# Ten pairs of projection blocks by Strassen's seven products, in a fused mLSTM, attention and feed-forward step

## The chip, the cores and the metric

The kernel runs on one core of one Trainium2 chip. TensorE (PE) multiplies, VectorE (DVE), ScalarE (ACT) and GpSimd (POOL) do the element-wise work, and SyncE (SP) issues most DMAs. Products are accumulated in PSUM; ACT and DVE read them from there. The metric is the device time of one launch, in microseconds (us), as the median of several runs. Times inside a launch come from one execution recorded by the hardware profiler.

## What is computed

One step of a hybrid decoder layer, for a prompt of 1024 tokens and a sample group of 8 x 4 tokens (1056 columns in all), with a model width of 1024. Cut to what matters:

```python
h = _ln(x) * (1.0 + sc1) + sh1
z = h @ w_in + b_in                       # one projection of all kinds
qm, km, vm, ig, fg, og, qa, ka, va, gm, ga = _split(z, IN_SPLITS)
hm, C, n, m = _mlstm(qm, km, vm, ig, log_sigmoid(fg), C0, n0, m0)   # 4 heads, chunks of 128 tokens
hm = _ln(hm) * mlstm_norm_w * sigmoid(og)
ha, k_new, v_new = _swa(qa, ka, va, kbuf, vbuf, pos0, sinks)        # 16 heads, window 128
merged = sigmoid(gm) * (hm @ w_branch_m) + sigmoid(ga) * (ha @ w_branch_a)
x = _ln(ALPHA * x + g1 * (merged @ w_out), ln1_g, ln1_b)
h2 = _ln(x) * (1.0 + sc2) + sh2
f, cbuf_new = _conv_ffn(h2, cbuf, w_up, b_up, conv_w, conv_b, w_down, b_down)
x = _ln(ALPHA * x + g2 * f, ln2_g, ln2_b)
# in _mlstm, per chunk: smat = (q k^T) * exp(dmat - mt); num = smat v + a_in * (C q); C = decay * C + k^T (ws v)
```

All data are float32.

## The kernel before

**Products.** Features stand on the partitions and tokens along the free axis. A block is 128 output features over all 1056 tokens. `group` (L442) makes the products of a block for one token tile of `TT` (384, 384 and 288 columns). Weights and activations are each split into two fp32r parts, hi and lo, and of the four partial products three are made (hi hi, hi lo, lo hi): for eight slices of the contraction 24 matmuls for a tile, 72 for a block. `Stream` (`win`) loads the weights of coming blocks on SP (`wraw`, L403), and ACT (L424) and DVE (L428) split them.

**Phases.** Phase A: the projection, 52 blocks of the kinds k, q, v, og (mLSTM), qa, ka, va (attention), gm, ga (branch gates) and the narrow gate rows. Phase B: two branch products and the output product. Phase C: feed-forward, `up` blocks and `down` blocks, where DVE adds each down group to a sum in SBUF (L1680). Some later stages follow.

**Side work.** mLSTM (a generator `mlstm(h)` for each head), attention (`swa_pair`, `swa`) and gate arithmetic are steps in the queue `sides`. `group` calls `pulse` after each slice; `pulse` advances a clock of products' time and takes a step from the queue whenever clock times rate (`RATES`) says so. A step issues all its instructions on every engine at once, so its PE instructions stand in one piece between two slices of a block. `finish_sides` takes all that are left, with nothing between them, before the last block of phase A. `later` puts off a DMA by some of that clock.

**PSUM.** It has eight tiles of 512 columns: `L[0..2]` for the direct groups, handed out in turn by `lbank`; `PD[0..1]`, `PE_`, `PF` and `PG` for side work. In an mLSTM step, chunk s is prepared in `PE_` (scores `k q`, L799, and three transposes), read by DVE and ACT (L804 to L810); `hn` (L751) of chunk s-2 is read by ACT out of `PD[(s-2) % 2]`; `hn` of s-3 is transposed into `PG` and multiplied by DVE (L824); the products of s-1 (L789) go to `PD[(s-1) % 2]` and `PF`. In an attention step the scores of two heads go to `PD[0]`, of two to `PD[1]` (L1137), each copied by ACT (L1142) and DVE (L1143); exponentials on ACT (L1122) of the step before stand ahead of these copies. An instruction that writes a tile waits, by semaphores that the framework puts in, for those that still read it.

**Slots.** SBUF has 43 slots of 128 x 1056 floats, handed out in the order in which they came back; an instruction that takes a slot waits for its last user.

Of the kernel before, what the change touches and what calls it, by code (L numbers as in the profile page):

```python
# [11 lines left out]
F32 = mybir.dt.float32  # L12
# [38 lines left out]
# columns of the table of constants  # L51
# [52 lines left out]
def hybrid_step(ctx: ExitStack, tc: tile.TileContext, I, O):  # L104
# [25 lines left out]
    def drop(*ts):  # L130
        for t in ts:
            free_slots.append(tag_of.pop(id(t))[0])
# [57 lines left out]
    # the rows of c in pieces of 128  # L190
# [7 lines left out]
    # vectors along the features, transposed: 0.. b_in (16 + 36 blocks), 52.. b_ada, 100.. norm_w,  # L198
    # 108.. b_down, 116.. b_up, 160.. conv_b, 204.. conv_w (3 x 44)
# [22 lines left out]
    def ada_load(ca, cb, f0, n=256):  # L222
        """Features f0 .. f0 + n of the factors ca and cb: their weights."""
        out = []
        for c in (ca, cb):
            for hf in range(2):
                if n > 128 or not hf:
                    t = slot(name="wada")
                w = t[:, hf * 512:hf * 512 + 512] if n == 128 else t[:, :1024]
                S.dma_start(w.rearrange("p (k c) -> p k c", k=4),  # L230
                            dap(W_ADA, hf * 4 * 128 * 6 * D + c * D + f0,
                                [[6 * D, 128], [128 * 6 * D, 4], [1, n]]))
                out.append((t, w))
        return out
# [32 lines left out]
    # silu(c), transposed  # L267
# [109 lines left out]
    def h_lo(k, ti, eng):  # L377
        t0, nt = TT[ti]
        hi, lo = acts[k]
        c = slice(t0, t0 + nt)  # L380
        eng.tensor_tensor(lo[:, c], h_f[k][0][:, c], hi[:, c].bitcast(F32), op=OP.subtract)
        h_f[k][1] += 1
        if h_f[k][1] == 3:
            drop(h_f.pop(k)[0])

# [1 line left out]
    class Stream:  # L387
        def __init__(self, specs):
            self.specs = specs
            self.raws, self.parts, self.loaded = {}, {}, 0  # L390

        def load(self, upto):
            while self.loaded <= min(upto, len(self.specs) - 1):
# [12 lines left out]
                self.loaded += 1  # L406

        def prep(self, i, later_lo=False):
            if i >= len(self.specs) or i in self.parts:
                return  # L410
# [43 lines left out]
    # ================= phase A: the combined projection, mLSTM, window attention =================  # L454
# [11 lines left out]
    for h in range(4):  # L466
        blk("k", h, 512 + 128 * h)
        blk("q", h, 128 * h)
        if h == 0:
            order.append(("gate", 0))  # L470
            specs.append(("gate",))
        blk("v", 2 * h, 1024 + 256 * h)
        blk("v", 2 * h + 1, 1024 + 256 * h + 128)
        blk("og", 2 * h, 2056 + 256 * h)
        blk("og", 2 * h + 1, 2056 + 256 * h + 128)
    gates = [("gm", j, 4616 + 128 * j) for j in range(8)] + [("ga", j, 5640 + 128 * j) for j in range(8)]
    gates = deque(gates)

    def add_gates(n):
        for _ in range(n):  # L480
            blk(*gates.popleft())
# [5 lines left out]
    blk("ka", 0, 4104)  # L487
    blk("va", 0, 4360)
    add_qa(0)
    add_gates(3)  # L490
    add_qa(1)
    add_gates(2)
    blk("ka", 1, 4104 + 128)
    blk("va", 1, 4360 + 128)
    add_qa(2)
    add_gates(4)
    add_qa(3)
    add_gates(7)

    # the order of all later products: branches, output product, feed-forward  # L500
# [25 lines left out]
    win = Stream(specs)  # L526

    # the first products take the chunks of h as they come
# [64 lines left out]
    # later constants  # L593
    v2, v3, v4 = slot(name="v2"), slot(name="v3"), slot(name="v4")
    rows(v2, 0, I["b_up"], 0, 44)
    rows(v2, 44, I["conv_b"], 0, 44)
    rows(v3, 0, I["conv_w"], 0, 88)
    rows(v4, 0, I["conv_w"], 88 * 128, 44)
# [7 lines left out]
    def late_consts():  # L606
        transpose(PF[:, 0:88], v2[:88, :128], 88)
# [105 lines left out]
    def cache_load(p):  # L713
        """The cached keys and values of a pair of groups."""
# [21 lines left out]
    def norm_tail(num, den, ecol, n):  # L736
        """The layer norm of num / max(|den|, e): its factor is (var(num) + eps max(|den|, e)^2)^-0.5."""
# [37 lines left out]
        # operands in two parts: q, v with a column of ones, the scores and the weighted keys  # L775
# [68 lines left out]
        # the state after the prompt  # L844
# [6 lines left out]
        # the sample group: all its tokens as one block  # L851
# [145 lines left out]
    def swa(g):  # L997
# [37 lines left out]
        def sample():  # L1035
            """The sample group: its rows are (sequence, head, token)."""
# [158 lines left out]
    def gate_rows_in(i):  # L1195
        """The gates' rows: products with both parts of the weights side by side, then their sum."""
# [47 lines left out]
    for h in range(4):  # L1244
        after["og", 2 * h + 1] = [lambda h=h: mlstm(h)]
    after["og", 7].append(state_n_out)
# [5 lines left out]
    def raw_pieces(src, ti):  # L1252
        """Loads a token tile of eight blocks that wait in DRAM."""
# [10 lines left out]
    def refill(raws, ti):  # L1264
        """Puts a token tile into the operand tiles, whose old contents its products have used."""
# [9 lines left out]
    rate[0] = RATES[0]  # L1275
    for i, (kind, idx) in enumerate(order):
        last = i == len(order) - 1
        if (kind, idx) == ("k", 1):
            rate[0] = RATES[1]
        if (kind, idx) == ("ka", 0):  # L1280
            rate[0] = RATES[2]
# [25 lines left out]
    # ================= phase B: branches and output product =================  # L1307
# [192 lines left out]
    # ================= phase C: the convolutional feed-forward =================  # L1500
# [14 lines left out]
    def conv_piece(c, y, a, b, w0):  # L1515
        """The prompt's columns a..b of the convolution of block c."""
# [20 lines left out]
    def post(c):  # L1537
        """Convolution, then gelu or the product, of a block that is complete."""
# [22 lines left out]
    def post_now(c, ti):  # L1561
        """The same for the last block, a token tile at a time."""
# [16 lines left out]
    def history():  # L1579
        """What the convolution reads of earlier steps, by feature; space for what it keeps."""  # L1580
# [24 lines left out]
    def pre():  # L1605
        """ALPHA x and the gated sums of all groups but the last, by tokens, into DRAM."""
# [26 lines left out]
        # the last gate along the features, on every token's partition: the prompt's, the samples'  # L1633
# [18 lines left out]
    def spread(gen, us):  # L1652
        """The steps of gen, one every us of the products' time."""
# [31 lines left out]
    # the first blocks take the token tiles in the order in which their norms end  # L1685
# [201 lines left out]
```

## Time and profile before

| | us |
|---|---|
| median of 3 runs | 1983.2 |
| the runs | 1982.83 to 1986.43 |
| span of the profiled execution | 1981.8 |
| PE busy in it | 1942.6 (98%) |
| DVE busy | 997.7 (50%) |
| ACT busy | 723.3 (36%) |
| POOL busy | 308.9 (16%) |

The profiled execution's span lies 1.4 us under the median. Names such as `L450` are lines of the kernel before; `L` among the tiles, as in `L<-hhi,whi`, is any of the three direct banks. The ends of matmuls are modelled, so spacings are read from start to start. [...]

### The profile page before, as it was taken

What the parts mean: (1) busy time and instruction counts of PE and PEld (TensorE: products, weight loads), DVE (VectorE), ACT (ScalarE), POOL (GpSimd) and SP (SyncE); (2) the same over time, 40 slices, a digit from 0 to 9 for tenths busy, and PEclk for the clock granted to TensorE, in tenths of its full rate; (3) what the DMA queues carried; (4) which work ended last, traced back from release to release, by engine and by line L of the source; (5) the groups of instructions that cost most, each with busy time, mean ns of one, the idle gap of its engine ahead of it and who ended that gap; (6) DMA issues with size and microseconds to landing.
All of it is one profiled execution on the core that took longest, in us unless ns stands there. A gap on an engine that the chain in (4) does not pass through costs nothing. (4 is left out here: it accounts for less than half of the span.)

```text
span 1981.8 us, 31279 instructions
## 1 busy us (share of the span) xinstructions
PE 1942.6 (98%) x12597; PEld 1858.1 (94%) x12597; DVE 997.7 (50%) x2166; ACT 723.3 (36%) x1522; POOL 308.9 (16%) x592
## 2 busy tenths in 40 slices
PE   6999999999999999999999999999999999999996
PEld 4899999999998989999999999999999999999995
DVE  4454444444544535241454455564554554645579
ACT  4534334343546445331312454353131312222331
POOL 2013223231123131200000333100000000000007
PEclk9999999999999999999999999999999999999998
DMA  9151424324220322497524142111212020211533
GB/s 289 47 140 25 140 35 119 84 70 100 69 76 23 112 72 60 136 345 244 159 65 128 54 129 67 36 38 48 60 35 62 28 69 27 63 34 49 194 130 130
DMA packets 214362, 187.86 MB, mean 95 GB/s; under 512 B 8849, under 2 KB 197953, under 8 KB 214185
## 3 DMA queue, kind: packets, MB, share of 16 engines
q1 hardware_dynamic: 213437, 185.26, 31.1%
q8 instruction: 98, 1.61, 0.3%
q10 hardware_dynamic: 780, 0.61, 0.1%
q14 instruction: 47, 0.39, 0.1%
HBM read 150.06 MB, written 37.81 MB: 95 GB/s over the span
## 5 line engine op out<-in xcount | busy, mean ns | idle before, releaser
L450 PE MATMUL L<-hhi,whi 128*128 128x384 f32 (+1 forms) x1600 | 526.4, 329 | 0.1
L450 PE MATMUL L<-hlo,whi 128*128 128x384 f32 (+1 forms) x1600 | 517.0, 323 | 0.0
L450 PE MATMUL L<-hhi,wlo 128*128 128x384 f32 (+1 forms) x1600 | 516.5, 323 | 0.0
L450 PE MATMUL L<-mhi,whi 128*128 128x384 f32 (+1 forms) x1248 | 407.4, 326 | 4.9 <-DVE r L1466 3.0
L450 PE MATMUL L<-mhi,wlo 128*128 128x384 f32 (+1 forms) x1248 | 404.1, 324 | 0.4 <-DVE wlo L428 0.4
L450 PE MATMUL L<-mlo,whi 128*128 128x384 f32 (+1 forms) x1248 | 403.3, 323 | 0.0
L428 DVE TENSOR_TENSOR wlo<-wraw,whi 128x1024 fp32r<-128x1024 f32 (+1 forms) x148 | 174.5, 1180 | 331.3 <-ACT whi L424 330.8
L450 PEld LDWEIGHTS L<-hhi,whi 128*128 128x128 f32 x1600 | 301.5, 188 | 6.6 <-issue 4.8
L450 PEld LDWEIGHTS L<-hlo,whi 128*128 128x128 f32 x1600 | 301.9, 189 | 0.3
L450 PEld LDWEIGHTS L<-hhi,wlo 128*128 128x128 f32 x1600 | 301.4, 188 | 0.0
L450 PEld LDWEIGHTS L<-mhi,whi 128*128 128x128 f32 x1248 | 235.4, 189 | 6.7 <-DVE r L1466 3.3
L450 PEld LDWEIGHTS L<-mhi,wlo 128*128 128x128 f32 x1248 | 234.9, 188 | 1.0 <-DVE wlo L428 1.0
L450 PEld LDWEIGHTS L<-mlo,whi 128*128 128x128 f32 x1248 | 235.3, 189 | 0.1
L1511 ACT ACTIVATE u<-L,vT 128x384 f32<-128x384 f32 (+1 forms) x132 | 71.8, 545 | 378.6 <-PE L L450 378.6
L424 ACT CAST whi<-wraw 128x1024 fp32r<-128x1024 f32 (+1 forms) x148 | 149.2, 1009 | 28.3 <-DMA wraw<-in_w_up 25.3
L450 PE MATMUL L<-ahi,whi 128*128 128x384 f32 (+1 forms) x432 | 139.9, 324 | 0.0
L450 PE MATMUL L<-ahi,wlo 128*128 128x384 f32 (+1 forms) x432 | 139.4, 323 | 0.0
L450 PE MATMUL L<-alo,whi 128*128 128x384 f32 (+1 forms) x432 | 139.3, 323 | 0.0
L1524 DVE SCALAR_TENSOR_TENSOR y<-u,vT,y 128x1023 f32<-128x1023 f32 (+3 forms) x92 | 113.7, 1235 | 2.5
L1534 POOL COPY ucol<-u 128x2 f32<-128x2 f32 x44 | 10.3, 234 | 631.7 <-ACT u L1511 631.7
L1680 DVE TENSOR_TENSOR facc<-L,facc 128x384 f32<-128x384 f32 (+1 forms) x120 | 62.7, 522 | 58.6 <-PE L L450 58.4
L298 POOL TENSOR_SCALAR rstd<-mv 128x1 f32<-128x1 f32 (+1 forms) x36 | 22.0, 611 | 400.6 <-DVE mv L307 377.2
(422 smaller groups left out, 2652.4 us busy)
## 6 DMA issues: line engine op xcount, KB each, us to landing
wraw<-in_w_in SPq DMA_DIRECT2D x52, 512.0 KB
wada<-in_w_ada SPq DMA_DIRECT2D x44, 512.0 KB
wraw<-in_w_up SPq DMA_DIRECT2D x44, 512.0 KB
wraw<-in_w_down SPq DMA_DIRECT2D x24, 384.0 KB
hD<-og SPq DMA_DIRECT2D x8, 528.0 KB
gmD<-gm SPq DMA_DIRECT2D x8, 528.0 KB
haD<-ha SPq DMA_DIRECT2D x8, 528.0 KB
gaD<-ga SPq DMA_DIRECT2D x8, 528.0 KB
```

The source lines that it names most:

```text
L298: G.tensor_scalar(r[:n], var, eps, None, op0=OP.add)
L424: A.copy(hi[:, :n], t[:, :n])
L428: V.tensor_tensor(lo[:, :n], t[:, :n], hi[:, :n].bitcast(F32), op=OP.subtract)
L450: T.matmul(ps[:, :nt], x[:, c], y[:, t0:t0 + nt], start=i == 0, stop=i == last)
L1511: A.activation(u[:, t0:t0 + n], ps[:, :n], AF.Identity, bias=b)
L1524: V.scalar_tensor_tensor(y[:, f:b], u[:, f - d:b - d], w[i], y[:, f:b], op0=OP.mult, op1=OP.add)
L1534: G.tensor_copy(aux["ucol"][:, c, 0:2], u[:, SEQ - 2:SEQ])
L1680: V.tensor_tensor(fx, ps[:, :nt], fx, op=OP.add)
```

## The change

Twenty blocks (four of gm, eight v, eight og) are no longer made directly. They are taken in ten pairs of two neighbouring blocks, and a pair is one 2 x 2 block product (two output blocks, even and odd slices of the contraction, two halves of the tokens) by Strassen's scheme in Winograd's form: seven products of half size instead of eight, over sums of weights (`Pair.step`, DVE) and of activations (`tprep`). Each product is 24 matmuls of 264 columns into each half of one PSUM tile; DVE and ACT add the products up out of PSUM (U1 to U5, `put`). To that end PSUM is now four tiles of 1024 columns, and the old banks are their halves.

The order is new: four gm blocks directly, the ten pairs (`fast`), the gate rows, then 28 direct blocks (k and q of the heads with ga blocks between, ka, va, qa), beside which all of mLSTM and attention runs at one rate. v and og are stored to DRAM after their pair (`pD`) and loaded again by `mlstm(h)`.

```diff
-    L = [psum.tile([128, 512], F32, name=f"L{i}") for i in range(3)]
-    PD = [psum.tile([128, 512], F32, name=f"PD{i}") for i in range(2)]
-    PE_, PF, PG = (psum.tile([128, 512], F32, name=f"P{i}") for i in "EFG")
+    BK = [psum.tile([128, 1024], F32, name=f"B{i}") for i in range(4)]
+    L = [BK[0][:, :512], BK[0][:, 512:], BK[1][:, :512]]
+    PD = [BK[2][:, :512], BK[2][:, 512:]]
+    PE_, PF, PG = BK[1][:, 512:], BK[3][:, :512], BK[3][:, 512:]
...
+    PAIRS = [(kind, 2 * j, c0 + 256 * j) for kind, c0, js in (("gm", 4616, range(NG // 2, 4)), ("v", 1024, range(4)),
+                                                              ("og", 2056, range(4))) for j in js]
...
     def mlstm(h):
-        qT, kT, vT0, vT1, og0, og1 = proj["q", h], proj["k", h], proj["v", 2 * h], proj["v", 2 * h + 1], \
-            proj["og", 2 * h], proj["og", 2 * h + 1]
+        qT, kT = proj["q", h], proj["k", h]
+        vT0, vT1, og0, og1 = (slot(name=k) for k in ("v", "v", "og", "og"))
+        for t, key in ((vT0, ("v", 2 * h)), (vT1, ("v", 2 * h + 1)), (og0, ("og", 2 * h)), (og1, ("og", 2 * h + 1))):
+            S.dma_start(t, pD[key])
         E, qA = slot(name="E"), slot(name="qA")
...
+        def step(self, i):
+            if i == 0:
+                self.sums = [slot(name="fsum") for _ in range(2)]
+                self.sum(1, self.q(1, 0), self.q(1, 1), OP.add)
+                self.sum(3, self.q(0, 0), self.q(1, 0), OP.subtract)
+            elif i == 1:
+                self.sum(2, self.s(1), self.q(0, 0), OP.subtract)
+                self.sum(4, self.q(0, 1), self.s(2), OP.subtract)
+                self.pa = self.parts(self.raw[0])
...
+        def product(self, p):
+            ps = banks2[0].rearrange("p (g x) -> p g x", g=2)[:, :, :HT]
+            banks2.rotate(-1)
+            for g in range(2):
+                for kp in range(4):
+                    (wh, wl), (xh, xl) = self.weights(p, kp), operand(p, kp, g)
+                    for i, (x, y) in enumerate(((wh, xh), (wh, xl), (wl, xh))):
+                        T.matmul(ps[:, g], x, y, start=kp == 0 and i == 0, stop=kp == 3 and i == 2)
+                pulse(1.45)
+            if p == 1:
+                A.copy(U1, ps)
+            elif p == 2:
+                self.put(0, 0, ps, U1)
+            elif p == 6:
+                V.tensor_tensor(U2, ps, U1, op=OP.add)
...
+    def fast(pairs, at_end):
+        prev = None
+        t1_split()
+        for n, pr in enumerate([*pairs, None]):
+            nxt = pairs[n + 1] if n + 1 < len(pairs) else None
+            for pos, p in enumerate((1, 3, 6, 2, 7, 4, 5)):
+                who = prev if p == 3 else pr
...
+    rate[0] = RATES[0]
+    sides.append(tprep())
+    for i in range(NG):
+        if i == NG - 1:
+            pairs[0].load()
+        direct(i)
+        if i == NG - 2:
+            finish_sides()
...
+    fast(pairs, at_end)
+    drop(hf[0], hf[2], *t3s, *b12)
+    late_loads()
+    rate[0] = 0.56
+    for i in range(NG, len(order)):
+        direct(i)
```

The same place in PE's order of before and of the change, three times. Rows give line, operation, written tile, operands and columns; in brackets stands the engine whose instruction is waited for. Tile names have lost a digit: `B_71` is the first 1024-column tile (L0 and L1), `B_72` the second (L2 and PE_), `B_73` the third (PD), `B_74` the fourth (PF and PG).

First, PE between the second and the third token tile of an up block in phase C. Before:

```order
L450 MATMUL L_71<-mhi_10401,whi_12860 128x384
L450 MATMUL L_71<-mlo_10402,whi_12860 128x384
L450 MATMUL L_71<-mhi_10401,wlo_12861 128x384
L450 MATMUL L_72<-mhi_9745,whi_12860 128x288 [waits Activation_49]
L450 MATMUL L_72<-mlo_9746,whi_12860 128x288
```

The wait is for ACT's reading of `L_72` three groups ago. After the change:

```order
L448 MATMUL B_71<-mlo_10914,whi_13452 128x384
L448 MATMUL B_71<-mhi_10913,wlo_13453 128x384
L448 MATMUL B_71<-mhi_10257,whi_13452 128x288 [waits Activation_49]
L448 MATMUL B_71<-mlo_10258,whi_13452 128x288
L448 MATMUL B_71<-mhi_10257,wlo_13453 128x288
```

Both groups now write one tile, and the wait names ACT's reading of the group that stands just ahead.

Second, PE in an mLSTM step of head 0 (transposes of `hn`, then the chunk's products). Before:

```order
L196 MATMUL PG<-cst,hn 128x128 [waits DVE_49,Activation_49]
L196 MATMUL PG<-cst,hn 128x128
L789 MATMUL PD_74<-vx_1326,wx_1327 128x258 x2
L789 MATMUL PD_74<-vx_1326,wx_1327 128x258 [waits Pool_49]
L789 MATMUL PF<-vx_1326,wx_1327 128x258 [waits DVE_49]
L789 MATMUL PF<-vx_1326,wx_1327 128x258 x2
```

After the change:

```order
L197 MATMUL B_74<-cst,hn 128x128 [waits DVE_49]
L197 MATMUL B_74<-cst,hn 128x128
L807 MATMUL B_73<-vx_3495,wx_3496 128x258 [waits Activation_49]
L807 MATMUL B_73<-vx_3495,wx_3496 128x258
L807 MATMUL B_73<-vx_3495,wx_3496 128x258 [waits Pool_49]
L807 MATMUL B_74<-vx_3495,wx_3496 128x258 [waits DVE_49]
L807 MATMUL B_74<-vx_3495,wx_3496 128x258 x2
```

The first product now waits for ACT (`hn` of the chunk before, out of the other half), and those into PF wait for the DVE instruction that reads the transposes in PG.

Third, PE in an attention step (scores of two heads, then of two more). Before:

```order
L1137 MATMUL PD_74<-khi_5151,q_243_5176 128x256 [waits DVE_49]
L1137 MATMUL PD_74<-klo_5152,q_243_5176 128x256
L1137 MATMUL PD_74<-khi_5151,q_244_5180 128x256
L1137 MATMUL PD_74<-klo_5152,q_244_5180 128x256
L1137 MATMUL PD_75<-khi_5151,q_245_5210 128x256 [waits DVE_49]
L1137 MATMUL PD_75<-klo_5152,q_245_5210 128x256
```

After the change:

```order
L1155 MATMUL B_73<-khi_6508,q_362_6524 128x256 [waits DVE_49]
L1155 MATMUL B_73<-klo_6509,q_362_6524 128x256
L1155 MATMUL B_73<-khi_6508,q_363_6528 128x256
L1155 MATMUL B_73<-klo_6509,q_363_6528 128x256
L1155 MATMUL B_73<-khi_6508,q_365_6547 128x256 [waits DVE_49]
L1155 MATMUL B_73<-klo_6509,q_365_6547 128x256
```

The second wait of before is for the masked copy of `PD_75` one step ago; that of the change is for the masked copy of the scores made just ahead.

## Rows read from the trace of the kernel before

**Rows 1.** the page: span; busy us (share of span), instructions of each engine.
```profile
span 1981.8 us, 31279 instructions
...
PE 1942.6 (98%) x12597; PEld 1858.1 (94%) x12597; DVE 997.7 (50%) x2166; ACT 723.3 (36%) x1522; POOL 308.9 (16%) x592
```

**Rows 2.** windows, 80 to 860 us: window, length, busy us, PEclk, DMA share, GB/s.
```profile
80.00:860.00 780.00, 779.87 (x5258) 741.19 (x5257) 372.61 (x1173) 355.42 (x944) 179.62 (x320) 1.00 0.32 88
```

**Rows 3.** timeline: start, length (us), engine, line, operation, tiles; spacings of matmuls.
```profile
1400.62 0.34 PE L450 MATMUL L<-ahi,whi 128*128 128x384 f32 x1
1400.80 0.34 PE L450 MATMUL L<-alo,whi 128*128 128x384 f32 x1
...
531.83 0.28 PE L1137 MATMUL PD<-klo,q 128*128 128x256 f32 x1
532.53 0.28 PE L1137 MATMUL PD<-klo,q 128*128 128x256 f32 x1
```

**Rows 4.** the page's costliest groups: split of weights (busy us, mean ns).
```profile
L428 DVE TENSOR_TENSOR wlo<-wraw,whi 128x1024 fp32r<-128x1024 f32 (+1 forms) x148 | 174.5, 1180 | 331.3 <-ACT whi L424 330.8
```

**Rows 5.** timeline, head 1: E issued on SP, the step on PE.
```profile
209.75 1.40 SPq L757 DMA_DIRECT2D E<-mD  x1
...
229.98 0.38 PE L799 MATMUL PE<-q,k 128*128 128x128 f32 x2
```

**Rows 6.** timeline: an evacuation that PE waits for, and one that it doesn't.
```profile
1213.43 0.56 ACT L1511 ACTIVATE u<-L,vT 128x384 f32<-128x384 f32 x1
1213.51 0.34 PE L450 MATMUL L<-mhi,wlo 128*128 128x384 f32 x1
1214.04 0.44 PE L450 MATMUL L<-mhi,whi 128*128 128x384 f32 x1 [0.20 <-ACT u L1511]
1214.32 0.34 PE L450 MATMUL L<-mlo,whi 128*128 128x384 f32 x1
...
1407.95 0.34 PE L450 MATMUL L<-ahi,wlo 128*128 128x384 f32 x1
1408.13 0.29 PE L450 MATMUL L<-ahi,whi 128*128 128x288 f32 x1
1408.26 0.29 PE L450 MATMUL L<-alo,whi 128*128 128x288 f32 x1
1408.33 0.56 DVE L1680 TENSOR_TENSOR facc<-L,facc 128x384 f32<-128x384 f32 x1 [1.02 <-PE L L450]
```

**Rows 7.** timeline: the step of mLSTM head 2 at 342.08.
```profile
342.08 0.60 PE L789 MATMUL PD<-vx,wx 128*128 128x258 f32 x3
343.36 0.56 ACT L751 ACTIVATE hn<-PD,mden 128x256 f32<-128x256 f32 x1
343.74 0.48 DVE L824 TENSOR_TENSOR og<-PG,og 128x128 f32<-128x128 f32 x2
```

**Rows 8.** timeline: two steps in close succession; the attention step at 793.11.
```profile
522.94 0.28 PE L1137 MATMUL PD<-khi,q 128*128 128x256 f32 x1
...
526.94 0.28 PE L1137 MATMUL PD<-khi,q 128*128 128x256 f32 x1
...
793.11 0.28 PE L1137 MATMUL PD<-khi,q 128*128 128x256 f32 x1
795.03 0.62 ACT L1142 COPY scr<-PD 128x256 f32<-128x256 f32 x2
795.41 0.46 DVE L1143 COPY_PREDICATED scr<-cst,PD 128x256 f32<-128x256 int32 x1 [2.59 <-ACT scr L1142]
```

**Rows 9.** windows of 4 us: busy us of PE first, PEclk third from last.
```profile
1160.00:1164.00 4.00, 1.69 (x13) 1.46 (x11) 2.72 (x4) 1.15 (x2) 3.73 (x5) 1.00 0.36 119
1164.00:1168.00 4.00, 3.27 (x15) 3.27 (x16) 2.92 (x5) 0.95 (x3) 3.20 (x4) 0.65 0.72 221
1208.00:1212.00 4.00, 2.89 (x17) 2.63 (x16) 2.09 (x4) 1.32 (x2) 3.73 (x4) 1.00 0.17 68
1212.00:1216.00 4.00, 3.80 (x22) 3.32 (x20) 0.65 (x2) 3.69 (x5) 1.26 (x4) 1.00 0.59 160
```

More of the change, by code (lines that the diff above doesn't have):

```diff
@@ L1244, in hybrid_step @@
     for h in range(4):
-        after["og", 2 * h + 1] = [lambda h=h: mlstm(h)]
-    after["og", 7].append(state_n_out)
+        after["q", h] = [lambda h=h: mlstm(h)]
+    after["q", 3].append(state_n_out)
     after["va", 0] = [lambda: swa_pair(0)]
@@ new lines, in t1_split, with operand @@
+    def t1_split():
+        for kp in range(4):
+            hi, lo = (quarters(t)[:, :, 1, :] for t in acts[2 * kp])
+            x = quarters(hf[2 * kp])[:, :, 0, :]
+            A.copy(hi, x)
+            V.tensor_tensor(lo, x, hi.bitcast(F32), op=OP.subtract)
+        drop(hf[4], hf[6])
+    def operand(p, kp, g):
+        e, o = 2 * kp, 2 * kp + 1
+        if p in (1, 2, 3, 5):
+            k, half_ = {1: (e, 0), 2: (o, 0), 3: (o, 1), 5: (e, 1)}[p]
+            return tuple(quarters(t)[:, g, half_, :] for t in acts[k])
+        if p == 7:
+            return tuple(t[:, g, :] for t in t3_ops[kp])
+        return tuple(quarters(t)[:, g, 0 if p == 4 else 1, :] for t in t_ops[kp])
@@ new lines, in fast @@
+    def fast(pairs, at_end):
[5 more added lines that the diff above has]
+                who = prev if p == 3 else pr
+                if who is not None:
+                    who.product(p)
+                if p == 3 and prev is not None:
+                    drop(*prev.ps[1])
+                if pr is None:
+                    if pos == 1:
+                        return
+                    continue
+                if pos == 0:
+                    pr.step(2)
+                elif pos == 1:
+                    pr.step(3)
+                    pr.step(4)
+                elif pos == 2 and nxt is not None:
+                    nxt.load()
+                elif pos == 3:
+                    drop(*pr.pa)
+                elif pos == 4 and nxt is not None:
+                    nxt.step(0)
+                elif pos == 5:
+                    drop(pr.pq)
+                    if nxt is not None:
+                        nxt.step(1)
+                elif pos == 6:
+                    drop(*pr.ps[0])
+                if nxt is None:
+                    at_end(pos)
+            prev = pr
@@ new lines, in hybrid_step, with finisher, finish, out @@
+    pD = {}
+    def finisher(kind, idx):
+        def finish(blk_, z):
+            j = idx + blk_
+            if kind != "v":
+                A.activation(z, z, AF.Tanh, scale=0.5)
+                f = hnw[:, j:j + 1] if kind == "og" else 0.5
+                V.tensor_scalar(z, z, f, f, op0=OP.mult, op1=OP.add)
+            t = dram.tile([128, TOK], F32, name=f"{kind}D{j}")
+            (gD if kind == "gm" else pD)[kind, j] = t
+            def out():
+                S.dma_start(t, z)
+                drop(z)
+            later(2.0, out)
+        return finish
@@ L1277, in hybrid_step, with direct @@
+    pairs = []
+    for kind, idx, c0 in PAIRS:
+        base = {"v": VB_V, "og": VB_OG, "gm": VB_GM}[kind] + idx
+        pairs.append(Pair((WIN, DIN, c0), finisher(kind, idx), [vT[:, base + i:base + i + 1] for i in range(2)]))
+    def direct(i):
+        kind, idx = order[i]
         last = i == len(order) - 1
[L1278 to L1281, printed above, removed]
         if last:
@@ L1305, in hybrid_step, with at_end @@
             sides.append(fn())
+    rate[0] = RATES[0]
[6 more added lines that the diff above has]
+            finish_sides()
+    pairs[0].step(0)
+    pairs[0].step(1)
+    b12 = []
+    def at_end(pos):
+        win.limit = len(specs)
+        if pos == 2:
+            win.load(NG)
+        elif pos == 3:
+            for i in range(2):
+                t = slot(name="b12")
+                b12.append(t)
+                for j in range(2):
+                    S.dma_start(t[:, j * 528:j * 528 + 528].rearrange("p (g n) -> p g n", g=2), b12D[2 * i + j])
+        elif pos == 4:
+            win.prep(NG)
+            win.load(NG + 1)
+        elif pos == 6:
+            drop(*(t for kp in range(4) for t in t_ops[kp]))
+            win.prep(NG + 1)
+            for kp in range(4):
+                hi, lo = (quarters(t)[:, :, 1, :] for t in acts[2 * kp])
+                x = b12[kp // 2][:, kp % 2 * 528:kp % 2 * 528 + 528].rearrange("p (g n) -> p g n", g=2)
+                A.copy(hi, x)
+                V.tensor_tensor(lo, x, hi.bitcast(F32), op=OP.subtract)
+    fast(pairs, at_end)
[4 more added lines that the diff above has]
+        direct(i)
     def gate_load(kind, j):
```

165 lines of the change are left out of this document (131 added, 34 removed).

## The prediction

> **What bounds the kernel now.** I read the page first: of a span of 1981.8 us TensorE (PE) is busy 98%, VectorE (DVE) 50%, ScalarE (ACT) 36%, GpSimd (POOL) 16% [rows 1]. From 80 to 860 us, where the projection blocks run with mLSTM and attention beside them, PE has work for 779.87 of 780 us at a granted clock of 1.00 [rows 2]. The list of PE's waits has `L450` waiting for evacuations `L1511` or `L1464` four times in the span; one of them, 0.20 us at 1214.04, is below [rows 6]. So time is the number of matmuls times their spacing, plus every wait that a change puts into PE's queue. PE runs its instructions in order: a wait in one holds all behind it.
>
> **Products.** A direct block is 24 matmuls for each of three token tiles. Successive starts lie 0.175 us apart at 384 columns [rows 3] and 0.13 at 288 (1408.13 and 1408.26 [rows 6]), so a block takes 24 x (2 x 0.1755 + 0.131) = 11.57 us. The change takes 20 of them out (231.4 us) and puts 10 x 168 = 1680 matmuls of 264 columns in. The trace has none of that size; the nearest are 256 columns (531.83 to 532.53, six steps: 0.117 [rows 3]). By 0.1755/384 a column they take 0.1204 us, together 202.3 us: **-29 us**. Both ends: 0.117 gives -35, 0.123 gives -25.
>
> [...]
>
> **The work around the pairs** (20 + 36 + 24 = +80 us). The first product over sums of weights waits for four DVE sums and a split (the split of a whole block takes DVE 1.18 us behind ACT's copy [rows 4]) and for the last of `tprep`: 10 us at the start, 0.4 us for each pair, 3 for refilling the operand tiles before the gate rows, 3 for the gate rows, of which nothing now lies between the exponentials and their transposes: 20. Each head now loads v and og (4 x 528 KB) and puts them on SP's queue ahead of E and qA. Before, E was issued at 209.75 and the first step that needs it (`L799`) ran at 229.98 [rows 5], 20 us later, which PE filled with blocks; now six loads of such size must land. For head 0 I take 16 us of waiting, for the other three 20 together: 36, from 0 if the loads come in time to 55. The side work no longer fits beside the blocks that are left: some ten steps of the last attention group run in `finish_sides` with no product between them. Where such steps follow each other closest they lie 4.0 us apart (522.94 to 526.94 [rows 8]), and one holds some 2 us of PE: 22 us with the first one's start, and 2 for what comes after at a lower clock; 10 to 35.
>
> **The halves of PSUM.** This is the largest part. The banks were eight tiles; now they are halves of four tiles. The order of PE's instructions with their waits says that the program guards the whole tile: 530 waits of PE name an instruction that reads or writes the other half of the tile, against 3 before. L0 and L1 are the halves of one tile, and `lbank` hands them out one after the other. So the first matmul of every group into L1 waits until the evacuation of the group just before it has ended; on PE only a side step could come between.
>
> The price is in the trace, since before has the same kind of wait a few times. At 1213.51 starts a group's last 384-column matmul; an evacuation 1213.43 to 1213.99 must end; the next matmul starts at 1214.04 and the one after it 0.28 us later instead of 0.175 [rows 6]. The handover costs 0.05 us and the restart 0.10. What the evacuation itself costs: a last matmul at 1407.95 has its evacuation from 1408.33 to 1408.89, while the next group began at 1408.13 [rows 6]; it would have had to wait 0.76 us. Over all 155 places of before where a 384-column group is followed by a 288-column one (1407.95 is one) the evacuation ends 0.78 us (median) after the next group's start, with a mean of 1.19 in the projection blocks, where ACT has other work, 0.77 in the branches, 0.85 in the up and 0.79 in the down blocks. With 0.15 each: 31 such groups in the projection at 1.34, 24 at 0.92 in the branches and output product, 44 at 1.00 up, 48 at 0.94 down: 41.5 + 22 + 44 + 45 = **+153 us**. Bounds: 147 x 0.76 = 112, and 190 if ACT, which has denser side work now, is late more often.
>
> *mLSTM steps.* The products of a chunk (`L789`) go to one PD half while `hn` (`L751`) of the chunk before reads the other, and PF's products stand behind `L824`, which reads PG, the other half of their tile. In the step at 342.08 the products start at 342.08, `hn` ends at 343.92, `L824` at 344.22 [rows 7]. In before that is free; now PE stands from 342.08 until 343.92, and there are 28 such waits. Over the 28 steps the end of `hn` lies 1.7 to 3.3 us behind the first product, 2.25 on average: **+63 us**. Behind the waiting matmul stand PF's products and the next direct group, so nothing covers it.
>
> *Attention steps.* The scores of two heads go to one PD half, those of the other two to the other half, which now waits for the masked copy of the first. At 793.11 the fifth matmul starts; the copy `L1142` begins at 795.03 behind exponentials, and the first of two masked copies `L1143` ends at 795.87, 2.76 us after that matmul's start [rows 8]. Over 32 steps the mean is 2.14 (0.2 to 3.6). 22 steps beside blocks at 2.15, and 10 in the tail, where the chain hides part, at 1.2: **+59 us**.
>
> *The rest.* L2 and PE_ share a tile too: some 50 waits of either direction, 0.3 to 1.2 us; 0.6 is the handover of one evacuation: +30. Sample steps, PV products and the last product over 512 columns: some 25 waits of about 1 us, +25.
>
> **The clock.** [...] A window of 4 us at 0.65 loses 1.4 us of PE: 0 to 70, I take 30.
>
> Sum: -29 + 80 + 153 + 63 + 59 + 55 + 30 = +411; 1981.8 + 411 = 2393. The span is 1.4 us under the median of 1983.2, and I forecast **2390 us**. Its own range: with the low bounds (-35 + 40 + 112 + 48 + 40 + 25 + 0 = +230) 2213, with the high ones (-25 + 115 + 190 + 80 + 75 + 85 + 70 = +590) 2573; not all fall to one side, so 2240 to 2500.
>
> **Rivals.**
> A: the waits between halves are there but mostly met when PE comes to them. Then only the work around the pairs counts: 1981.8 - 29 + 80 + 1.4 = 2034. For it speaks that such waits were short in before (0.20 us at 1214.04 [rows 6]); against it that there the reader was that of three groups ago, not of the last. [...] The order shows that the program waits all the same, and no row of before can show two halves. 6%.
>
> B, faster: the waits cost nothing, the loads of v and og come in time (the DMA engines are busy 0.32 of this stretch [rows 2]), and the rate of 0.56 drains the side work before the last block. Of the work around the pairs the 0.4 us for each pair stay: 1981.8 - 29 + 4 + 1.4 = 1958. It decides where evacuations end before the next group's first matmul; 1408.89 against 1408.13 [rows 6] speaks against it. 4%.
>
> C: the clock falls at most waits of 2 us and in the blocks too, which stand 0.9 in 11.6 us. 147 more falls of 1.4 us would add 206: some 2600. The 1.00 of 1208 to 1216 [rows 9] speaks against it. 6%.
>
> D: the pairs don't do what they say: DVE cannot keep up with sums, splits and seven evacuations for a pair. A pair has three and a half splits of 1.18 us [rows 4], four sums of half that size and eight readings of 528 columns, some 12 us of DVE in 20.2; it would take 40% more to bind, and add some 50 us to the forecast. 4%, inside the range.
>
> The forecast has 80%, spread over its range. 2230 to 2510 leaves out A, B, C and the forecast's ends: about 2 in 10. Between 1979.2 and 1987.2 (0.2%, what a measurement of this kernel can tell from no change) I leave 1%; faster 4%, slower 95%.
>
> **What would show it.** Right: PE's list of waits after has `L448` behind evacuations for 130 to 180 us; a 288-column group starts about 0.95 us behind the last 384-column matmul in every down block; `L807` into PD waits for ACT about 2 us in 28 steps, `L1155` for DVE in 32. PE is busy about 80% of a span of 2390. `L1421` matmuls lie 0.120 us apart, and the stretch of the ten pairs takes 205 to 225 us. Wrong: PE still 95% busy, or groups into L1 starting 0.18 us behind the last matmul; then the halves are free and A or B holds. If the span is near 2390 with PE's waits elsewhere (E, wraw), the sum is right for the wrong reason.

## The result and the profile after

The changed kernel takes 2494.6 us (median of 4 runs, 2490.3 to 2503.8) against 1984.8 us for the kernel before: a ratio of 1.258, 95% interval 1.255 to 1.261. 2390 us was forecast, with a range of 2230 to 2510. The direction, the place and the mechanism were right; the time is 105 us longer than forecast. One term of the sum explains that, the clock: it cost some 117 us more than was taken for it, while the waits came out 34 us lower.

The page of the changed kernel: span, then busy time and instructions of each engine [rows 1].

```profile
span 2488.6 us, 32079 instructions
PE 2088.4 (84%) x12837; PEld 1919.4 (77%) x12837; DVE 1114.4 (45%) x2304; ACT 745.2 (30%) x1520; POOL 298.6 (12%) x592
```

PE was idle 39.2 us of its span before and is idle 400.2 us now, and it is busy 146 us longer although it has less to multiply. The rest of the reading is about these two numbers: 361 us of waits, and 146 us in which the same work takes longer.

PE's list of waits in the changed kernel (engine, tile, line, what it waits for: us in total, times, longest). `B` is any of the four tiles.

```profile
PE B L1155 <- DVE scr L1161: 74.0, 33, 4.3
PE B L807 <- ACT hn L767: 48.8, 28, 3.1
PE B L448 <- ACT u L1785: 37.0, 40, 9.2
PE B L448 <- DVE facc L1954: 27.5, 40, 1.2
PE B L817 <- ACT ga L1198: 18.5, 1, 18.5
PE B L448 <- ACT r L1738: 11.8, 5, 9.1
PE B L448 <- ACT ga L1198: 11.6, 8, 4.1
PE B L448 <- DVE r L1740: 10.9, 3, 9.3
```

The first two and most of the `L448` rows are waits that the kernel before does not have. `L1785` (up) and `L1954` (down) are evacuations, the reading of a finished group out of PSUM, for which a direct group now waits 40 times each. One such place, in an up block (timeline: start, length, engine, line, operation, tiles; in brackets the idle time before and what ended it):

```profile
1903.80 0.34 PE L448 MATMUL B<-mhi,wlo 128*128 128x384 f32 x1
1904.18 0.58 ACT L1785 ACTIVATE u<-B,vT 128x384 f32<-128x384 f32 x1 [3.56 <-PE B L448]
1904.81 0.40 PE L448 MATMUL B<-mhi,whi 128*128 128x288 f32 x1 [0.67 <-ACT u L1785]
1905.05 0.29 PE L448 MATMUL B<-mlo,whi 128*128 128x288 f32 x1
```

The evacuation ends at 1904.76 and the next group starts at 1904.81, 1.01 us behind the last matmul of the one before. At the like place of before it was 0.18 us [rows 6]. Over the 135 places of this trace where a 288-column group follows a 384-column one, the distance is 1.008 us in the median, against 0.175 before.

An mLSTM step and an attention step (timelines of the changed kernel), to be read beside [rows 7, 8]:

```profile
512.04 0.58 ACT L767 ACTIVATE hn<-B,mden 128x256 f32<-128x256 f32 x1
512.67 0.98 PE L807 MATMUL B<-vx,wx 128*128 128x258 f32 x6 [2.71 <-ACT hn L767]
...
1063.02 0.28 PE L1155 MATMUL B<-klo,q 128*128 128x256 f32 x1
1065.07 0.36 ACT L1160 COPY scr<-B 128x256 f32<-128x256 f32 x1
1065.46 0.44 DVE L1161 COPY_PREDICATED scr<-cst,B 128x256 f32<-128x256 int32 x1 [2.58 <-ACT scr L1160]
1065.96 0.39 PE L1155 MATMUL B<-khi,q 128*128 128x256 f32 x1 [2.65 <-DVE scr L1161]
```

In both the PE instruction starts 0.05 to 0.06 us after the reader of the other half has ended.

Last, the table by stretches of the changed kernel (window, length, busy time of PE, PEld, DVE, ACT and POOL, PEclk, DMA share, GB/s): pairs, mLSTM, attention, branches, feed-forward. PEclk is the clock granted to PE as a share of full speed; in the traces of before and of the change it is either 1.00 or 0.50, and 0.50 is called half clock.

```profile
100.00:340.00 240.00, 220.27 (x1713) 216.10 (x1714) 138.93 (x183) 62.20 (x77) 0.31 (x1) 0.96 0.32 95
340.00:760.00 420.00, 303.46 (x1734) 274.69 (x1732) 161.13 (x472) 126.72 (x306) 96.33 (x208) 0.88 0.30 87
760.00:1200.00 440.00, 334.49 (x1916) 283.50 (x1915) 165.29 (x614) 172.86 (x535) 74.09 (x113) 0.84 0.16 47
1200.00:1442.00 242.00, 224.16 (x1464) 204.37 (x1464) 87.76 (x167) 47.81 (x88) 0.00 (x0) 0.99 0.54 174
1442.00:2414.00 972.00, 875.22 (x5282) 838.79 (x5281) 455.70 (x668) 277.84 (x426) 73.56 (x192) 0.98 0.19 59
```

The feed-forward in the kernel before, same columns:

```profile
1065.00:1915.00 850.00, 844.52 (x5286) 838.48 (x5285) 451.02 (x665) 276.17 (x424) 74.79 (x192) 1.00 0.22 67
```

Of the 507 us, 122 come in the feed-forward (849.4 us before, from 1065.9 to 1915.3, and 971.8 now), whose products the change does not touch; some 370 between the first blocks and the end of the branches. From 340 to 1200 us PE is idle a quarter of the time and its clock is at 0.88 and 0.84, where it was 1.00 [rows 2].

### The profile page after: what moved, and what is told of

It reads as the page before. It is cut to its first block, busy times and chain, and to the rows that moved or that the text cites. A ratio compares the mean times of both kernels' runs of the same rounds, so it can differ in the third digit from the quotient of the medians.

```text
span 2488.6 us, 32079 instructions
## 1 busy us (share of the span) xinstructions
PE 2088.4 (84%) x12837; PEld 1919.4 (77%) x12837; DVE 1114.4 (45%) x2304; ACT 745.2 (30%) x1520; POOL 298.6 (12%) x592
## 5 line engine op out<-in xcount | busy, mean ns | idle before, releaser
L448 PE MATMUL B<-mhi,whi 128*128 128x384 f32 (+1 forms) x1248 | 415.4, 333 | 62.5 <-ACT u L1785 37.0
L448 PE MATMUL B<-hhi,whi 128*128 128x384 f32 (+1 forms) x1120 | 399.2, 356 | 75.0 <-ACT ga L1198 11.6
L448 PE MATMUL B<-mlo,whi 128*128 128x384 f32 (+1 forms) x1248 | 406.2, 326 | 0.0
L448 PE MATMUL B<-mhi,wlo 128*128 128x384 f32 (+1 forms) x1248 | 406.0, 325 | 0.0
L448 PE MATMUL B<-hlo,whi 128*128 128x384 f32 (+1 forms) x1120 | 382.2, 341 | 0.0
L448 PE MATMUL B<-hhi,wlo 128*128 128x384 f32 (+1 forms) x1120 | 381.4, 341 | 0.0
L448 PEld LDWEIGHTS B<-hhi,whi 128*128 128x128 f32 x1120 | 230.3, 206 | 100.6 <-ACT ga L1198 14.6
L448 PEld LDWEIGHTS B<-mhi,whi 128*128 128x128 f32 x1248 | 237.5, 190 | 79.2 <-ACT u L1785 49.9
L448 PEld LDWEIGHTS B<-mlo,whi 128*128 128x128 f32 x1248 | 237.5, 190 | 0.1
L448 PEld LDWEIGHTS B<-mhi,wlo 128*128 128x128 f32 x1248 | 237.2, 190 | 0.0
L448 PEld LDWEIGHTS B<-hlo,whi 128*128 128x128 f32 x1120 | 231.1, 206 | 0.3
L448 PEld LDWEIGHTS B<-hhi,wlo 128*128 128x128 f32 x1120 | 229.2, 205 | 0.0
L1785 ACT ACTIVATE u<-B,vT 128x384 f32<-128x384 f32 (+1 forms) x132 | 71.9, 545 | 448.5 <-PE B L448 448.5
L448 PE MATMUL B<-ahi,whi 128*128 128x384 f32 (+1 forms) x432 | 144.9, 335 | 32.9 <-DVE facc L1954 27.5
L448 PE MATMUL B<-ahi,wlo 128*128 128x384 f32 (+1 forms) x432 | 139.6, 323 | 0.0
L448 PE MATMUL B<-alo,whi 128*128 128x384 f32 (+1 forms) x432 | 139.5, 323 | 0.0
L448 PEld LDWEIGHTS B<-ahi,whi 128*128 128x128 f32 x432 | 81.2, 188 | 48.2 <-DVE facc L1954 40.3
L1954 DVE TENSOR_TENSOR facc<-B,facc 128x384 f32<-128x384 f32 (+1 forms) x120 | 62.8, 524 | 95.6 <-PE B L448 95.6
```

The lines of the kernel that those rows point to most:

```text
L448: T.matmul(ps[:, :nt], x[:, c], y[:, t0:t0 + nt], start=i == 0, stop=i == last)
L1785: A.activation(u[:, t0:t0 + n], ps[:, :n], AF.Identity, bias=b)
L1954: V.tensor_tensor(fx, ps[:, :nt], fx, op=OP.add)
```

## The experiments

The theory: PE waits for whoever reads the other half of a tile (so the PSUM tiles make the loss), and the low clock behind the longer waits adds to it. Rival 1: the denser packing of side work, the loads of v and og and the tail (attention steps with no blocks left beside them) make it. Rival 2 (within the theory): nearly all is the group waits.

**e1_split: the change with eight tiles.**

```diff
-    BK = [psum.tile([128, 1024], F32, name=f"B{i}") for i in range(4)]
-    L = [BK[0][:, :512], BK[0][:, 512:], BK[1][:, :512]]
-    PD = [BK[2][:, :512], BK[2][:, 512:]]
-    PE_, PF, PG = BK[1][:, 512:], BK[3][:, :512], BK[3][:, 512:]
+    L = [psum.tile([128, 512], F32, name=f"L{i}") for i in range(3)]
+    PD = [psum.tile([128, 512], F32, name=f"PD{i}") for i in range(2)]
+    PE_, PF, PG = (psum.tile([128, 512], F32, name=f"P{i}") for i in "EFG")
...
-    banks2 = deque(BK)
+    banks2 = deque([(L[0], L[1]), (L[2], PE_), (PD[0], PD[1]), (PF, PG)])
...
-                V.tensor_tensor(U2, ps, U1, op=OP.add)
+                for g in range(2):
+                    V.tensor_tensor(U2[:, g], ps[g], U1[:, g], op=OP.add)
```

> The change with PSUM as eight separate tiles of 512 columns again; each Strassen product is read out of two tiles by two instructions instead of one. Theory (waits for the other half of a tile, and the low clock behind them, make the loss): PE's waits L448 behind the evacuation of the group just before, L807 behind hn and L1155 behind the masked copy go, PE busy falls by the 147 us that the low clock costs, and the time is 2490 less 146 (group waits), 123 (mLSTM and attention waits), some 60 (other halves) and 140 (clock): 2000 to 2070 us. Rival 1 (the denser packing beside fewer blocks, the loads of v and og and the tail without blocks make the loss): it keeps most of it, 2350 to 2450 us. Rival 2 (two read-outs instead of one make the pairs bound by VectorE): the stretch of the pairs grows from 218 us to over 240.

Measured: 2121.2 us, 1.069 of before (1.067 to 1.071): 373 us of the 510 are gone. Its busy times on the page, and the largest of PE's waits:

```profile
PE 1975.8 (93%) x12837; PEld 1869.0 (88%) x12837; DVE 1117.9 (53%) x2374; ACT 739.2 (35%) x1530; POOL 302.7 (14%) x592
```

```profile
PE PE L816 <- DVE wx L827: 28.4, 7, 8.3
PE PF L1109 <- POOL scr L1120: 14.5, 12, 2.7
PE L L1420 <- ACT fhi L1377: 7.8, 2, 6.4
PE PE L196 <- DMA v<-vD: 7.6, 2, 6.8
PE PD L196 <- ACT gr L709: 6.1, 1, 6.1
```

Rival 1 does not hold: it would have kept most of the loss. The run's own rival, pairs bound by two read-outs, does not hold either: the pairs lie between 102 and 316 us. Rival 2 is not decided here, since all halves went at once. But 136 us stay, 51 more than the upper bound expected: PE is idle 104 us longer than before, and busy 33 us longer with 26 us less to multiply, at a granted clock of 0.965. Some 70 of the 104 us are waits for loads, tail and entry: heads' first steps and v (36 us), tail (15), entry, gate rows and exit (some 20). Most of the others are waits in attention and mLSTM steps (`L1154` 13.9 us, `L196` behind `hs` 5.4) and for weights of a later stage (`L240` behind `wada`, 7.2).

**e2_halves: before, with the halves alone.**

```diff
-    L = [psum.tile([128, 512], F32, name=f"L{i}") for i in range(3)]
-    PD = [psum.tile([128, 512], F32, name=f"PD{i}") for i in range(2)]
-    PE_, PF, PG = (psum.tile([128, 512], F32, name=f"P{i}") for i in "EFG")
+    BK = [psum.tile([128, 1024], F32, name=f"B{i}") for i in range(4)]
+    L = [BK[0][:, :512], BK[0][:, 512:], BK[1][:, :512]]
+    PD = [BK[2][:, :512], BK[2][:, 512:]]
+    PE_, PF, PG = BK[1][:, 512:], BK[3][:, :512], BK[3][:, 512:]
```

> The kernel before with nothing changed but the PSUM tiles: four of 1024 columns, the old banks their halves. Theory: some 170 group waits of 0.8 us with restart (136), three long ones behind the norms (27), 28 mLSTM steps of 1.8 (50), 32 attention steps of 2.3 (74), other halves 50, and the clock behind the long ones 100 to 150: 1983 + 340 to 490, that is 2320 to 2470 us. Rival 1 (packing and loads): under 2100 us, since packing is that of before. If the waits count but the low clock needs the denser packing: about 2300 us at a granted clock over 0.98.

Measured: 2398.4 us, 1.209 (1.206 to 1.211), inside the range expected; rival 1 (under 2100) is out. These four lines cost 413 us without any Strassen product, and they bring the list of the changed kernel:

```profile
PE B L1138 <- DVE scr L1144: 66.1, 32, 3.1
PE B L790 <- ACT hn L752: 43.2, 27, 2.2
PE B L451 <- ACT u L1512: 37.9, 40, 9.6
PE B L451 <- DVE facc L1681: 27.3, 40, 1.2
```

The two parts together (413 and 136) would make 549; the change lost 510. The waits for loads and in the tail are some 21 us shorter in the changed kernel than in e1 (`L817` 23.4 us where `L816` and v have 36.0; `L1110` 5.8 where `L1109` has 14.5). That fits a PE that comes later to a load when it has waited elsewhere, but no run tests it.

**e3_l01: before, with L0 and L1 as halves of one tile.**

```diff
-    L = [psum.tile([128, 512], F32, name=f"L{i}") for i in range(3)]
+    LL = psum.tile([128, 1024], F32, name="LL")
+    L = [LL[:, :512], LL[:, 512:], psum.tile([128, 512], F32, name="L2")]
```

> The kernel before with one change: L0 and L1 are halves of one PSUM tile, the other six banks are tiles of their own. Theory: only the group waits come, some 170 of 0.8 us and a few long ones: 1983 + 140 to 190 = 2120 to 2175 us, at a granted clock near 0.99, since waits of 0.7 us cost no clock. If the clock falls behind these short waits too: over 2250 us. Rival 2 (the group waits are nearly all of the loss of the change): 2300 us or more.

Measured: 2198.1 us, 1.108 (1.105 to 1.110): +213 us, above the range expected. Of the 413 us of e2 that is half, and under the 2300 us of rival 2, which is out. The clock behaved as expected. From 1400 to 1700 us, all up and down blocks, PE is busy 274 of 300 us and the clock stays at 1.00:

```profile
1400.00:1700.00 300.00, 273.75 (x1641) 261.63 (x1640) 141.98 (x196) 78.47 (x123) 7.30 (x42) 1.00 0.14 40
```

PE is idle 160 us longer and busy 54 us longer. Restarts behind some 165 waits are 17 of the 54 (the second matmul behind a wait comes 0.10 us late). Three waits of 9 us each (below) were not in my estimate, and the granted clock of the whole run is 0.985, where before has 0.995: 66 us, if taken at half clock (2195.9 x 0.015 x 2), in place of 20, which is 23 us of work. What the last 14 us or so of the 54 are I can't tell.

**e4_pd and e5_pd_fill: before, with PD0 and PD1 as halves of one tile; then the same with PE kept busy.** In e5 PE multiplies something that nobody uses while it would wait (the lines behind the first cut are of e5 alone).

```diff
-    PD = [psum.tile([128, 512], F32, name=f"PD{i}") for i in range(2)]
+    DD = psum.tile([128, 1024], F32, name="DD")
+    PD = [DD[:, :512], DD[:, 512:]]
...
+                if c:
+                    for _ in range(14):
+                        T.matmul(PF[:, 256:512], wh[b], vh[b][:, :256], start=True, stop=True)
                 prod(num, (smh[b], sml[b]), (vh[b], vl[b]), True, c == 0)
...
+                    if j2:
+                        for _ in range(18):
+                            T.matmul(PF[:, 512 - nk:512], q2[0][:, n * 128:(n + 1) * 128], khi[:, k0:k0 + nk],
+                                     start=True, stop=True)
```

> The kernel before with one change: PD0 and PD1 are halves of one PSUM tile. Theory: 28 mLSTM waits of 1.8 us and 32 attention waits of 2.3 us come, some 125 us of waiting, and behind most of them one window at half clock, 1.7 us of work lost each: 1983 + 125 + 60 to 100 = 2165 to 2210 us, granted clock 0.95 to 0.97. If the clock does not fall: 2105 us at 0.99. Rival 1: within 2000 us, because before has enough blocks around each step.

> The kernel before with PD0 and PD1 as halves of one tile (as in the run e4_pd, 2170 us), and ahead of each matmul that then waits 14 (mLSTM) or 18 (attention) matmuls of 256 columns whose results nobody uses, 1.6 and 2.1 us of PE work where PE stood idle. If the price of these waits beyond their own length (e4_pd: waits grew by 126 us, the time by 185) is the low clock that follows an idle PE: the waits are filled, the granted clock goes back to 0.99 and the time falls by 45 to 65 us, to 2105 to 2125, though there is more work. If it is not the clock: 2170 to 2190 us.

Measured: e4 2169.9 us, 1.094 (1.090 to 1.097); e5 2140.5 us, 1.079 (1.077 to 1.081). The stretch from 80 to 880 us of e4, then of e5:

```profile
80.00:880.00 800.00, 695.72 (x4336) 653.86 (x4334) 317.85 (x976) 291.66 (x753) 153.82 (x283) 0.94 0.24 64
```

```profile
80.00:880.00 800.00, 780.62 (x5350) 741.87 (x5348) 320.27 (x986) 301.29 (x779) 163.10 (x297) 0.99 0.25 67
```

In e4, within its range, the waits grow by 126 us (`L1138` 69.7 us in 32 waits, `L790` 46.6 in 28) and the time by 185. PE is also busy 66 us longer in the profiled execution: 110 us more at half clock are worth 55 of them, restarts behind 60 waits some 6. That is 0.9 us of lost work for each wait, where the expectation had put 1.7 behind most of them. In e5 968 extra matmuls (some 113 us) stand in these waits, the granted clock of the whole run is 0.992 in place of 0.970 (worth some 48 us of work), and the time falls by 29 us although PE has more to do. That is less than the 45 expected: the extra matmuls are longer than some of the waits, and 17 us of the two waits remain. So the price of an idle PE through its clock is shown, at 29 us or more for 60 waits of 2 us in a kernel like before.

**e6_E_first, e7_tail and e8_best: what is left in e1.** e6 puts the loads of E and qA ahead of those of v and og. e7 moves ga blocks to the end and takes a rate of 0.64. e8 loads the next head's tiles early, and splits the first pair earlier, with a rate of 0.6 beside the first four blocks. e7 contains e6, and e8 contains e7; the cuts stand in this order.

```diff
-        for t, key in ((vT0, ("v", 2 * h)), (vT1, ("v", 2 * h + 1)), (og0, ("og", 2 * h)), (og1, ("og", 2 * h + 1))):
-            S.dma_start(t, pD[key])
         E, qA = slot(name="E"), slot(name="qA")
         S.dma_start(E, dap(mD, h * TOK, [[0, 128], [1, TOK]]))
         S.dma_start(qA, dap(aD, h * TOK, [[0, 128], [1, TOK]]))
+        for t, key in ((vT0, ("v", 2 * h)), (vT1, ("v", 2 * h + 1)), (og0, ("og", 2 * h)), (og1, ("og", 2 * h + 1))):
+            S.dma_start(t, pD[key])
...
-    add_fill(1)
     add_kva(1)
     add_qa(2)
-    add_fill(1)
     add_qa(3)
-    add_fill(2)
+    add_fill(4)
...
+        if h < 3:
+            fetch(h + 1)
...
     for i in range(NG):
-        if i == NG - 1:
+        if i == NG - 2:
             pairs[0].load()
         direct(i)
         if i == NG - 2:
-            finish_sides()
-    pairs[0].step(0)
-    pairs[0].step(1)
+            pairs[0].step(0)
+            pairs[0].step(1)
+    finish_sides()
```

> The change with eight tiles (as e1_split, 2121 us), with E and qA loaded ahead of v and og of a head. If the waits at the first step of each head (L816 28 us and the transposes of v 8 us in e1_split) are for E behind the four loads: 15 to 25 us less, 2095 to 2106 us, what is left being v, which then lands last. If the loads as a whole (six of 528 KB) set it: 2115 to 2125.

> e6_E_first with three ga blocks moved to the end and a rate of 0.64 in place of 0.56, so that no attention step is left to be drained without blocks beside it. In e1_split the drained stretch from 900 to 960 us lost some 20 us of waiting and ran at a clock of 0.78. Theory: 25 to 35 us less than e6_E_first, near 2070. Rival (denser steps bring as many new waits as the tail loses): within 8 us of e6_E_first.

> e7_tail with E, qA, v and og of the next head loaded when the chunks of a head are done, and the first pair's weights and sums and the sums of activations made beside the first four blocks. If the rest over the kernel before is waiting for loads and for DVE at the entry, and the low clock behind it: 2030 to 2050 us. The products' own saving of 26 us would need all of it gone, 1960 us; I do not expect that.

Measured: e6 2096.2 us (1.056, 1.054 to 1.058), e7 2103.3 (1.060, 1.058 to 1.062), e8 2101.5 (1.060, 1.058 to 1.061). e6 gave 25 us, its upper end, so the wait for E behind the four loads was real: `L816` falls from 28.4 to 5.9 us, and what is left is v (13.9 for 7.6). e7 gave nothing: its rival holds. The drained stretch went, with 9 of the 16 us of `L1109`, but PE is idle 128 us in all, as in e6: the wait for weights of a later stage stays (`wada`, 11.5 us where e6 has 12.1), and the denser steps brought waits of their own. e8's early loads took nothing off either, and its 2030 to 2050 was missed: `L821` waits 13.5 us and v 8.7, where e6 had 5.9 and 13.9. No version here beats the kernel before.

**e9_pairing: the change, with other partners in a tile.**

```diff
-    L = [BK[0][:, :512], BK[0][:, 512:], BK[1][:, :512]]
-    PD = [BK[2][:, :512], BK[2][:, 512:]]
-    PE_, PF, PG = BK[1][:, 512:], BK[3][:, :512], BK[3][:, 512:]
+    L = [BK[i][:, :512] for i in range(3)]
+    PD = [BK[i][:, 512:] for i in range(2)]
+    PE_, PF, PG = BK[3][:, :512], BK[3][:, 512:], BK[2][:, 512:]
```

> The change with its four tiles of 1024 columns and nothing else altered than which old banks share one: L0 with PD0, L1 with PD1, L2 with PG, PE_ with PF. Consecutive direct groups and consecutive chunks then write different tiles. Theory (each wait costs what its reader still has to do): the 147 group waits and the 28 and 32 waits behind hn and the masked copy go, but PF's products now wait for the split of PE_ (1.3 us, 28 times), some 26 direct groups for attention's masked copies (1 to 2 us), 16 for the reading of PG, and 28 transposes for the copy out of PF (0.5 us): 2121 (separate tiles) + 36 + 40 + 15 + 15 and 30 for the clock = 2230 to 2290 us. If only group waits mattered: under 2150. If any sharing costs the same: 2450 or more.

Measured: 2337.0 us, 1.179 (1.174 to 1.183): 158 us less than the change, 47 more than the upper end expected. Between 1700 and 1900 us, where only direct blocks run, nothing is lost now. The stretch in the changed kernel, then in e9:

```profile
1700.00:1900.00 200.00, 182.44 (x1093) 174.40 (x1092) 96.72 (x132) 56.95 (x90) 4.70 (x27) 1.00 0.14 41
```

```profile
1700.00:1900.00 200.00, 200.00 (x1244) 200.00 (x1243) 103.76 (x149) 47.95 (x75) 5.76 (x33) 1.00 0.15 46
```

1244 matmuls in place of 1093 in the same time. Beside the side work other waits take their place: `L807` behind the split of PE_, `L197` behind the copy out of PF (where I had 15), `L448` behind attention's masked copies.

```profile
PE B L807 <- DVE wx L828: 38.2, 28, 2.7
PE B L197 <- ACT ha L1114: 28.9, 28, 2.3
PE B L448 <- DVE scr L1161: 24.2, 14, 2.8
```

In all PE is idle 156 us longer than in e1, where 106 was taken, and the clock stays low (0.947): 248 us at half clock, 100 more than in e1 and so 50 us of work, where 30 was taken. With separate tiles PE has none of these three.

## Why the prediction came out as it did

**Products: right.** The 1680 matmuls lie 0.122 us apart (0.1204 was taken), 205 us for 231: -26 in place of -29. (0.1755/384 a column gives 0.1207 us at 264, not the 0.1204 of the prediction; the sum stays at -29.) The ten pairs take 218 us from their first matmul to their last; 205 to 225 was forecast. The rival of pairs that VectorE binds (D) is out: in the steady part PE waits twice, 0.17 us each, and DVE is busy 108.11 of the 180 us from 140 to 320, some 12.5 us a pair. Its 12 us in 20.2 would need two thirds more to bind, not the 40% of the prediction.

**Work around the pairs: right in its three parts, too low in all.** 20 + 36 + 24 = 80 was forecast. In e1, where the halves do not cover it, waits for loads are 36.0 us, the entry, gate rows and exit some 20, and the tail 15 in waits; but PE is idle 104 us longer than before, and the waits beyond these parts were not foreseen. In the changed kernel head 0 waits 18.5 us in one piece; 16 was taken. That the two are so close is in part luck, since the piece is not the load alone. SP takes 11.62 us to issue the two loads of v (from 379.63), so that E is issued only at 392.30 and DVE starts on it at 402.48. ACT's step on E (`L787`) ends at 405.23, and behind it in ACT's queue stands an evacuation of a ga block (`L1198`, 406.48 to 407.05), for which `L817` waits until 407.11. In e1, with separate tiles, the waits at this place are 6.8 us for v and 7.3 behind `wx`.

**Halves: right in mechanism and nearly in size.** 153 + 63 + 59 + 55 = 330 us were forecast, with some 15 of restarts. Groups: 0.83 us for each in the median and 0.10 of restart, where the sum had 0.89 on average and 0.15. mLSTM: 48.8 us in 28 waits (63 taken, from distances in a trace in which the step had no wait before it). Attention: 74.0 us in 33 (59 taken; the tail hid nothing). Three places of 9 us each were not foreseen: `L1738`, `L1740` and `L1785` behind the norms of a token tile. There the evacuation stands in ACT's queue behind steps of the norms (`L1647`) that start 4.65 to 4.71 us apart, each waiting for POOL; `L1740`, on DVE, waits for such an ACT evacuation. At 1493.63 the last matmul of a group starts, at 1502.45 its evacuation:

```profile
1493.63 0.34 PE L448 MATMUL B<-mhi,wlo 128*128 128x384 f32 x1
1502.45 0.56 ACT L1738 ACTIVATE r<-B,modT 128x384 f32<-128x384 f32 x1
1503.07 0.69 PE L448 MATMUL B<-mhi,whi 128*128 128x384 f32 x1 [9.10 <-ACT r L1738]
```

Before, the same delay cost 3.0 us at most, since a bank was asked for again only three groups later.

All idle time of PE grew by 361 us. Forecast were 80 + 330 less the restarts, 395. So the sum of the waits was right within 10%, somewhat too high.

**The clock: the step that failed.** The sum has 30 us for it, 0 to 70: at 1.4 us a window some 20 windows, at most 50. No run shows either count; in their place the trace of the change has the 44 falls counted below. PE's busy time grew by 146 us with 26 us less to multiply; less some 25 us of restarts this leaves about 147 us for the low clock, twice the upper bound. Rows of the changed kernel, 1064 to 1084 us, behind the wait of 2.65 us shown above:

```profile
1064.00:1068.00 4.00, 1.37 (x8) 1.05 (x8) 1.30 (x5) 2.38 (x10) 1.83 (x3) 0.90 0.00 0
1068.00:1072.00 4.00, 4.00 (x17) 2.86 (x17) 0.81 (x7) 0.00 (x0) 0.00 (x0) 0.50 0.00 0
1072.00:1076.00 4.00, 2.21 (x10) 1.68 (x8) 0.54 (x3) 2.74 (x12) 1.85 (x3) 0.74 0.00 0
1076.00:1080.00 4.00, 3.50 (x18) 3.50 (x19) 2.12 (x11) 0.37 (x1) 0.38 (x1) 0.68 0.00 0
1080.00:1084.00 4.00, 3.25 (x20) 2.13 (x19) 0.54 (x3) 1.82 (x8) 0.90 (x2) 0.89 0.00 0
```

I had priced each fall as one stretch of 4 us and then recovery, as in [rows 9]. Here the next wait comes before the clock is back, and the fall lasts. The trace has 44 falls to 0.50 (before has 4), 311 us in all: more than twice as many as the some 20 priced, and 3.5 us of lost work for each on average in place of 1.4. A granted clock of 0.938 over the run is 2488.6 x 0.062 x 2 = 309 us at half clock, where 0.995 before is 20. e5 shows that it is idleness that does it: with the waits filled, this goes from 130 us (0.970) in e4 to 34 (0.992). The short waits between blocks cost no clock: 1.00 from 1700 to 1900 us, with 17.6 us idle in 200, and so rival C is out. That 2494.6 us lies in the range at all is in part luck: the clock's own bounds did not hold it, and the room came from the other terms, the waits among them, which were put too high.

**Rival A** (waits mostly met when PE comes) is out by e2 and e3, **rival B** (faster) by all of it; e1 shows that even without the halves the change is 7% slower. The work around the pairs outweighs the 26 us saved, and the low clock behind its idle PE, with the restarts, costs another 59 us or so. In the prediction A gave 2034 us for this case; 2121 was measured, and again the missing part is mostly the clock (59 us), then waits (104 us for 80).

In the kernel before, where the direct banks are tiles of their own, two of them work side by side: a group runs from 1408.13 on while the one ahead of it is read, 1408.33 to 1408.89 [rows 6]. The changed program guards by tile, and the traces show that it pays for it: 0.67 us idle at 1904.81 for two halves of one tile.

## What to carry to other kernels

Before two buffers become views of one tile, ask who reads the one while the other is written: where dependencies are kept for the tile, a rotation over views is no rotation, and the order of instructions with its waits tells so without a run. Price an evacuation, not a semaphore: PE waits for what stands ahead of the reader in its queue and not only for its instruction (9 us at 1503). And where PE goes idle a few times in a row, add the clock to the wait: here about 147 us beside 361, as long as nothing else keeps PE busy.

## What the runs showed of the hardware that was not expected

After waits of 2 us the granted clock was not always lower. PE was busy 1.96 us of 508 to 512 and the next windows are at 1.00; from 1068 to 1072 it was at 0.50. Windows of the changed kernel:

```profile
508.00:512.00 4.00, 1.96 (x14) 1.72 (x12) 2.20 (x6) 2.45 (x7) 3.16 (x5) 1.00 0.46 143
512.00:516.00 4.00, 3.33 (x22) 3.33 (x23) 1.68 (x5) 1.09 (x4) 1.51 (x4) 1.00 0.41 123
516.00:520.00 4.00, 2.51 (x19) 2.23 (x18) 1.79 (x7) 1.29 (x4) 1.59 (x4) 1.00 0.00 0
```

So a single wait's price can't be read from its length; what the runs allow is the price of many (60 waits of 2 us in e4: 110 us more at half clock than before, and 29 us or more of time). A matmul behind a wait is followed by the next 0.24 us later in place of 0.13 at 288 columns (1904.81 and 1905.05): 0.1 us is lost at each restart, beside the wait itself.
